# First modulation of a decoder layer: weights of two d tiles in one load, the first pair's products on TensorE

## The chip, the cores and the metric

The kernel runs on one core of one Trainium2 chip. The metric is the device time of one execution in microseconds. TensorE multiplies matrices and transposes, VectorE and ScalarE work elementwise, GpSimd too but without access to the PSUM banks, and SyncE (SP) only issues transfers. Each engine takes its instructions in order.

## What is computed

One layer of a decoder with 1024 tokens, width 1024, f32, with a modulation of both norms:

```python
c_act = jax.nn.silu(c)
mod = (c_act @ mod_w[l] + mod_b[l])[:, None, :]
sh1, sc1, g1, sh2, sc2, g2 = jnp.split(mod, 6, axis=-1)
h = _rmsnorm(x, norm1_g[l]) * (1.0 + sc1) + sh1
z = h @ w_in[l]
q, k, v, f_logit, u = jnp.split(z, splits, axis=-1)
...   # attention with forget gates, pooling, output projection
h = _rmsnorm(x, norm2_g[l]) * (1.0 + sc2) + sh2
x = x + g2 * _conv_ffn(h, ...)
return _rmsnorm(x, final_g)
```

The change lies in how `sh1` and `sc1` (the columns g = 0 and g = 1 of `mod_w`, 1024 each) reach the first `h`, and in the order of the work around that.

## The kernel before

Accuracy of f32 is had with pairs: a matrix is split in a high part (a cast on ScalarE) and a low part (raw minus high), and each product is three matmuls, high by high, low by high, high by low.

The start-up stage (lines 123 to 456) turns x into `HI` and `LO`, the pair of the transposed, modulated `h`, and computes the first three column blocks of the projection (`psu`, one q, one k and one pooling block). x comes in eight tiles of 128 tokens (`load_x`). Per pair of tiles: squares on ScalarE (`norm_sq`), a root (`norm_pair`), scaling with VectorE for one tile and GpSimd for the other (`norm_scale`), 16 transposes into four PSUM banks (`norm_T(t)`, groups g of two d tiles), and copies into `xT[j]` (`norm_evac(t, g)`). There are eight d tiles j of 128 columns.

The modulation of d tile j is a column of `A1` (scale) and of `H1` (shift). `load_mod_d(j)` loads its weights as four transfers of 256 KB into two buffers `mst` (128 rows by 4 k by 2 g by 128 columns, so rows of 512 B in memory). `mod_dve(j, k0, k1)` multiplies and adds them over k on VectorE into `accd`, one operation of 256 elements a row for each k; `mod_end(j)` sums over the 128 partitions with two products of two columns on TensorE, and two activations on ScalarE write A1 and H1. For the tiles 0 and 1 the last two k (`NV` = 6) are products on TensorE instead (`mod_pe`).

`make_hT(j, ch)` makes one token half ch of tile j: ScalarE writes HI and an f32 copy `hf`, and `LOb` is their difference, on GpSimd for all tiles but the last (`LOJ` = 7) and the first half of tile 0. `su_mm(j, ch)` is the nine matmuls of 512 columns that use it. `su_split` splits the weights of these blocks (`sur` into `suh` and `sul`, the low part on GpSimd), in two halves of four k. `wv_gen` splits the weights of v (`wvr`, low part on GpSimd) for the next stage, `v_gen`, whose products are `psv`.

In this stage the order on TensorE, VectorE, ScalarE, GpSimd and SP is the order of the code (`manual_schedule`: `order`, `startup` and `loads`). `startup` ends at line 456; behind it a planner orders VectorE, ScalarE and GpSimd by its own timeline, and TensorE keeps the written order to the end. PSUM has eight banks, all under one tag (`B1`); six of them hold `psu` once both halves have begun. `warm` issues small products without use.

The loop over the d tiles (line 436) begins a tile's first product, ends the modulation of the next, sums the one after, and makes HI and LO of the next:

```python
for j in range(KT):
    if j > 0: su_mm(j, 0, (0,))
    if j + 1 < KT:
        mod_end(j + 1)
        if j + 2 < KT: mod_dve(j + 2)
    if j > 0: su_mm(j, 0, (1, 2))
    ...   # make_hT(j + 1, 0), make_hT(j + 1, 1), su_split, wv_gen
    su_mm(j, 1)
```

Of the kernel before, what the change touches and what calls it, by code (L numbers as in the profile page):

```python
# [50 lines left out]
def kernel(  # L51
# [115 lines left out]
    modv = mod_w.rearrange("(k p) (g j b) -> g j p k b", p=128, g=6, b=128)  # L167
    mst = {}

    def load_mod_d(j):  # L170

        st = []
        for hf in range(2):
            m = (Tqk if j < 4 else Tmx)("mst", (128, 4, 2, 128), F32)
            for g in range(2):
                nc.sync.dma_start(out=m[:, :, g, :], in_=modv[g, j][:, hf * 4:hf * 4 + 4, :])
            st.append(m)
        mst[j] = st
# [19 lines left out]
    for j in range(1, 4):  # L198
        load_mod_d(j)
# [75 lines left out]
    def norm_evac(t, g):  # L275
        for j in (2 * g, 2 * g + 1):
            if j not in xT:
                xT[j] = (Tp if j < 5 else Tv if j < 7 else Tqk)(f"xT{j}", (128, 1024), F32)
            o = xT[j][:, t * 128:(t + 2) * 128]
            i_ = nps[t, g][:, (j % 2) * 256:(j % 2) * 256 + 256]  # L280
            if g % 2 == 0 or t > 3:
                nc.scalar.copy(out=o, in_=i_)
            else:
                nc.vector.tensor_copy(out=o, in_=i_)
# [6 lines left out]
    def mod_pe(j):  # L291

        pm = pms[j] = B1("pm")
        for g in range(2):
            for k in range(NV, KT):
                mm(pm[:, 0:2], lhsT=mst[j][1][:, k % 4, g, :], rhs=cact[:, k, 1 - g:3 - g],
                   start=g == 0 and k == NV, stop=False)

    def mod_dve(j, k0=0, k1=KT):
        if k0 == 0:  # L300
            accs[j] = Ts2("accd")
        acc = accs[j]
        for k in range(k0, k1):
            m = mst[j][k // 4][:, k % 4]
# [6 lines left out]
    def mod_end(j):  # L311
        fresh = j not in pms
        pm = B1("pm") if fresh else pms[j]
        for g in range(2):
            mm(pm[:, 0:2], lhsT=accs[j][:, g, :], rhs=one_z[:, 1 - g:3 - g], start=fresh and g == 0, stop=g == 1)
# [4 lines left out]
    def Ts2(name):  # L320
        return Tpt(name, (128, 2, 128), F32)

    def make_hT(j, ch, eng):
# [20 lines left out]
    def wv_gen(vh, r):  # L344
# [3 lines left out]
        for k0 in range(0, KT, g):  # L348
# [5 lines left out]
            while a < k1:  # L354
# [4 lines left out]
                nc.gpsimd.tensor_sub(out=ll, in0=raw, in1=f(hh))  # L359
# [29 lines left out]
    for g in range(4):  # L389
        norm_evac(0, g)  # L390
    warm(WARM[2])
    norm_T(2)
    norm_sq(4)
# [3 lines left out]
    for g in range(4):  # L397
        norm_evac(2, g)
    warm(WARM[3])
    norm_T(4)  # L400
    norm_sq(6)
    norm_sq(7)
    mod_dve(0, 0, 4)
    norm_evac(4, 0)
    norm_evac(4, 1)
    norm_pair(6)
    norm_scale(6)
    warm(WARM[4])
    mod_pe(0)
    mod_dve(0, 4, NV)  # L410
    norm_evac(4, 2)
    norm_evac(4, 3)
    for i in range(3):
        su_split(i, 0, nc.gpsimd)
    norm_T(6, (0, 1))
    norm_evac(6, 0)
    mod_end(0)
    norm_T(6, (2, 3))
    mod_dve(1, 0, 4)
    make_hT(0, 0, nc.vector)  # L420
    for g in range(1, 4):
        norm_evac(6, g)
    su_mm(0, 0, (0,))
    mod_dve(1, 4, NV)
    mod_pe(1)
    su_mm(0, 0, (1, 2))
    make_hT(0, 1, nc.gpsimd)
    for i in range(3):
        su_load(i, 1)
    for j in range(4, KT):  # L430
        load_mod_d(j)
# [4 lines left out]
    for j in range(KT):  # L436
        if j > 0:
            su_mm(j, 0, (0,))
        if j + 1 < KT:
            mod_end(j + 1)  # L440
            if j + 2 < KT:
                mod_dve(j + 2)
        if j > 0:
            su_mm(j, 0, (1, 2))
        if j + 1 < KT:
            eng = nc.gpsimd if j + 1 < LOJ else nc.vector
            make_hT(j + 1, 0, eng)
            make_hT(j + 1, 1, eng)
        for i in {1: (0, 1), 2: (2,)}.get(j, ()):
            su_split(i, 1, nc.gpsimd)  # L450
# [1312 lines left out]
```

## Time and profile before

| | us |
|---|---|
| median of 3 runs (1107.68 to 1109.01) | 1108.06 |
| the profiled execution, its own time | 1108.36 |
| its span, first to last instruction | 1106.6 |
| TensorE busy in the span | 1071.8 |
| VectorE busy | 877.4 |
| ScalarE busy | 590.8 |
| GpSimd busy | 184.9 |

The profile names engines PE (TensorE matmuls), PEld (its weight loads), DVE (VectorE), ACT (ScalarE), POOL (GpSimd) and SP. An instruction is named by its line, operation and `out<-in` with the names of the tiles. Matmuls are pipelined, so the busy time of one is longer than its distance to the next. Times in the rows are microseconds from the start of the span.

### The profile page before, as it was taken

The numbers are of one execution on the slowest core, as the hardware profiler recorded it, in microseconds if no ns is written. First come the engines' busy times: TensorE is split into PE (matmuls) and PEld (weight loads), VectorE is DVE, ScalarE is ACT, GpSimd is POOL, SyncE is SP. The second block draws the span as 40 slices with busy tenths as digits, with TensorE's granted clock in tenths as the row PEclk, the third lists the DMA queues.
The fourth block names the chain that finished last, engine by engine and source line by source line (L and its number), as shares of the span: only waits on it lengthen the run. The fifth ranks groups of instructions, "written<-read, shape, count | busy, mean of one in ns | idle before, by whom it ended". The sixth has DMA issues, their size and how long they took to land.

```text
span 1106.6 us, 15492 instructions
## 1 busy us (share of the span) xinstructions
PE 1071.8 (97%) x5400; PEld 894.6 (81%) x5400; DVE 877.4 (79%) x1562; ACT 590.8 (53%) x1085; POOL 184.9 (17%) x185
## 2 busy tenths in 40 slices
PE   7899999989999999999999999999999999999997
PEld 7689887768877788888888888888888888788885
DVE  6987578878668645889877777788887869969986
ACT  7664445545667605766544545555655545425434
POOL 4565243336256510000000000000000000000000
PEclk9899999999999999999999999999999999999999
DMA  9953265371333612205322232324334289992474
GB/s 297 293 185 91 52 207 145 91 202 45 64 66 104 219 39 92 80 20 140 108 95 77 76 95 74 133 99 168 117 135 139 88 282 381 387 338 86 144 247 152
DMA packets 138389, 161.90 MB, mean 146 GB/s; under 512 B 9597, under 2 KB 94409, under 8 KB 138313
## 3 DMA queue, kind: packets, MB, share of 16 engines
q1 hardware_dynamic: 133561, 143.89, 41.8%
q10 hardware_dynamic: 4752, 17.04, 3.9%
q8 instruction: 42, 0.69, 0.3%
q14 instruction: 34, 0.28, 0.1%
HBM read 126.26 MB, written 30.45 MB: 142 GB/s over the span
## 4 chain that ended last, share of the span: by engine, by line
PE 76%; DVE 13%; DMA 4%; ACT 3%; issue 3%; POOL 0%; SPq 0%; DVEq 0%; ACTq 0%; POOLq 0%
PE ua L1297 19%; PE ub L1297 10%; PE da L1297 9%; PE db L1297 6%; PE z L923 5%; PE uc L1297 5%; DMA mrow<-in_mod_w_dram 3%; PE po L986 2%; PE po L984 2%; PE po L988 2%; PE psu L337 2%; PE pv L829 2%; DVE P L775 2%; PE psv L661 1%; PE psv L662 1%
## 5 line engine op out<-in xcount | busy, mean ns | idle before, releaser
L1262 ACT CAST uh<-wraw 128x512 fp32r<-128x512 f32 x128 | 79.2, 622 | 122.1 <-PE ua L1297 78.2
L1263 DVE TENSOR_TENSOR ul<-wraw,uh 128x512 fp32r<-128x512 f32 x128 | 87.5, 684 | 15.8 <-PE ub L1297 10.4
L1297 PE MATMUL ua<-t,uh 128*128 128x512 f32 x320 | 98.7, 390 | 0.3 <-ACT u L1341 0.3
L786 ACT ACTIVATE P<-P,mn 128x128 f32<-128x128 f32 (+3 forms) x64 | 49.7, 777 | 76.0 <-DVE mn L775 41.9
L793 POOL TENSOR_SCALAR P<-P,ri 128x128 f32<-128x128 f32 (+3 forms) x64 | 65.7, 1028 | 136.7 <-DVE ri L792 129.2
L810 DVE TENSOR_TENSOR pl<-tpp,ph 128x512 fp32r<-128x512 f32 (+1 forms) x80 | 50.7, 634 | 34.1 <-ACT ph L809 33.8
L1297 PEld LDWEIGHTS ua<-t,uh 128*128 128x128 f32 x320 | 59.9, 188 | 13.2 <-ACT u L1341 0.7
L1297 PE MATMUL da<-th,sl 128*128 128x512 f32 (+1 forms) x166 | 63.6, 383 | 1.6 <-DVE sl L1615 1.6
L775 DVE CUSTOM_DVE_ANT_0 P<-s,Fb 128x512 f32<-128x512 f32 (+2 forms) x96 | 50.2, 552 | 17.6 <-PE s L773 10.3
L1297 PE MATMUL da<-th,sh 128*128 128x512 f32 (+1 forms) x166 | 63.4, 382 | 0.5 <-DVE sv L1629 0.5
L1297 PE MATMUL da<-tl,sh 128*128 128x512 f32 (+1 forms) x166 | 63.3, 381 | 0.0
L1297 PE MATMUL ua<-t,ul 128*128 128x512 f32 x160 | 62.3, 389 | 0.0
L1297 PE MATMUL ua<-HIb,uh 128*128 128x512 f32 x160 | 62.2, 389 | 0.0
L1297 PE MATMUL ua<-LOb,uh 128*128 128x512 f32 x160 | 62.2, 389 | 0.0
L1297 PE MATMUL ua<-HIb,ul 128*128 128x512 f32 x160 | 62.2, 389 | 0.0
L923 PE MATMUL z<-HIb,wh 128*128 128x512 f32 x144 | 60.6, 421 | 0.0
L1374 DVE SCALAR_TENSOR_TENSOR tvv<-cv,colB,tvv 128x1023 f32<-128x1023 f32 (+1 forms) x44 | 56.2, 1279 | 5.2 <-ACT tvv L1372 4.8
L923 PE MATMUL z<-LOb,wh 128*128 128x512 f32 x144 | 59.4, 412 | 0.0
L923 PE MATMUL z<-HIb,wl 128*128 128x512 f32 x144 | 59.0, 409 | 0.0
L1374 DVE SCALAR_TENSOR_TENSOR tg<-cg,colB,tg 128x1023 f32<-128x1023 f32 (+1 forms) x44 | 56.3, 1279 | 1.0 <-ACT tg L1372 0.9
L809 ACT CAST ph<-tpp 128x512 fp32r<-128x512 f32 (+1 forms) x80 | 43.1, 540 | 20.5 <-PE tpp L802 9.7
L1297 PE MATMUL db<-th,sh 128*128 128x512 f32 x132 | 51.3, 389 | 0.0
(322 smaller groups left out, 3158.4 us busy)
## 6 DMA issues: line engine op xcount, KB each, us to landing
wraw<-in_ffn_up_dram SPq DMA_DIRECT2D x88, 256.0 KB, 3.4
mrow<-in_mod_w_dram SPq DMA_DIRECT2D x32, 512.0 KB, 8.3
actd<-tvv ACTq DMA_DIRECT2D x22, 512.0 KB, 2.7
ra<-in_ffn_down_dram SPq DMA_DIRECT2D x44, 256.0 KB, 5.3
x<-in_x_dram SPq DMA_DIRECT2D x16, 512.0 KB, 5.0
mst<-in_mod_w_dram SPq DMA_DIRECT2D x32, 256.0 KB, 5.4
ra<-actd SPq DMA_DIRECT2D x29, 256.0 KB, 5.7
rb<-in_ffn_down_dram SPq DMA_DIRECT2D x22, 256.0 KB, 5.2
```

Of the source, the lines that this page charges most:

```text
L337: mm(su_ps[i, ch], lhsT=su_w[i][w][:, j, :], rhs=act[j][:, ch * 512:(ch + 1) * 512], start=j == 0 and n == 0, stop=j == KT - 1 and n == 2)
L775: nc.vector.tensor_tensor_reduce(out=pt[:, n0:n1], in0=s[:, 0:n], in1=Fb[:, n0:n1], scale=1.0, scalar=3.0e38, op0=ALU.add, op1=ALU.min, ac ...
L786: nc.scalar.activation(out=pt, in_=pt, func=AF.Exp, scale=-1.0, bias=mn, accum_out=rs)
L793: nc.gpsimd.tensor_scalar(out=pt, in0=pt, scalar1=ri, scalar2=1.0, op0=ALU.mult, op1=ALU.mult)
L809: nc.scalar.copy(out=ph[:, 0:W], in_=tp[:, 0:W])
L810: nc.vector.tensor_sub(out=pl[:, 0:W], in0=tp[:, 0:W], in1=f(ph[:, 0:W]))
L829: mm(o, lhsT=V, rhs=x_[:, sl], start=b == 0 and not lo, stop=bool(lo and diag and kb == 1))
L923: mm(t[ch], lhsT=w[:, k, :], rhs=act[kk][:, ch * 512:(ch + 1) * 512], start=i == 0 and m == 0 and p0, stop=i == 1 and m == 3 and p1)
L1262: nc.scalar.copy(out=h, in_=src)
L1263: nc.vector.tensor_sub(out=l, in0=src, in1=f(h))
L1297: mm(*a, skip_group_check=True, **k)
L1374: nc.vector.scalar_tensor_tensor(out=t[:, sh:S], in0=s[:, 0:S - sh], scalar=cw_col[w][:, jj:jj + 1], in1=t[:, sh:S], op0=ALU.mult, op1=ALU ...
```

## The change

The first modulation is loaded for two d tiles at once: `load_mod_d(jp)` makes four buffers of the same size as before, 2 k by 2 g by 256 columns, two transfers of 256 KB each, with rows of 1 KB. The number of transfers and bytes stays. The first pair (tiles 0 and 1) has no sums on VectorE any more: all eight k are products on TensorE. For the other pairs VectorE sums six k in operations of 512 elements, and TensorE does two k and the sum over partitions, per tile. GpSimd does none of the splits of this stage: LO, the `sul` and the first `wvl` are subtractions on VectorE. Transposes are copied out of PSUM in another order and partly by another engine, tokens 0 to 511 first; two of the `warm` calls go; `su_mm(0, 0)` comes before the last transposes. The loop begins with tile 1 and ends the modulation of two tiles at every odd j. The diff:

```diff
@@ -164,18 +164,15 @@
         nc.scalar.copy(out=h, in_=raw)
         eng.tensor_sub(out=l, in0=raw, in1=f(h))
 
-    modv = mod_w.rearrange("(k p) (g j b) -> g j p k b", p=128, g=6, b=128)
+    modv = mod_w.rearrange("(k p) (g j b) -> g j p k b", p=128, g=6, b=256)
     mst = {}
 
-    def load_mod_d(j):
-
-        st = []
-        for hf in range(2):
-            m = (Tqk if j < 4 else Tmx)("mst", (128, 4, 2, 128), F32)
+    def load_mod_d(jp):
+
+        for q in range(4):
+            m = mst[jp, q] = (Tqk if jp < 2 else Tmx)("mst", (128, 2, 2, 256), F32)
             for g in range(2):
-                nc.sync.dma_start(out=m[:, :, g, :], in_=modv[g, j][:, hf * 4:hf * 4 + 4, :])
-            st.append(m)
-        mst[j] = st
+                nc.sync.dma_start(out=m[:, :, g, :], in_=modv[g, jp][:, 2 * q:2 * q + 2, :])
 
 
     wv_raw = {}
@@ -195,8 +192,7 @@
     load_mod_d(0)
     for i in range(3):
         su_load(i, 0)
-    for j in range(1, 4):
-        load_mod_d(j)
+    load_mod_d(1)
 
     def warm(n):
 
@@ -272,36 +268,39 @@
 
     xT = {}
 
-    def norm_evac(t, g):
+    def norm_evac(t, g, dve):
         for j in (2 * g, 2 * g + 1):
             if j not in xT:
                 xT[j] = (Tp if j < 5 else Tv if j < 7 else Tqk)(f"xT{j}", (128, 1024), F32)
             o = xT[j][:, t * 128:(t + 2) * 128]
             i_ = nps[t, g][:, (j % 2) * 256:(j % 2) * 256 + 256]
-            if g % 2 == 0 or t > 3:
+            if dve:
+                nc.vector.tensor_copy(out=o, in_=i_)
+            else:
                 nc.scalar.copy(out=o, in_=i_)
-            else:
-                nc.vector.tensor_copy(out=o, in_=i_)
 
     A1 = cp.tile([128, 8], F32, name="A1")
     H1 = cp.tile([128, 8], F32, name="H1")
 
     pms, accs = {}, {}
 
-    def mod_pe(j):
-
-        pm = pms[j] = B1("pm")
-        for g in range(2):
-            for k in range(NV, KT):
-                mm(pm[:, 0:2], lhsT=mst[j][1][:, k % 4, g, :], rhs=cact[:, k, 1 - g:3 - g],
-                   start=g == 0 and k == NV, stop=False)
-
-    def mod_dve(j, k0=0, k1=KT):
+    def mod_pe(j, k0=NV, k1=KT, last=False):
+
+        fresh = j not in pms
+        if fresh:
+            pms[j] = B1("pm")
+        b = slice((j % 2) * 128, (j % 2) * 128 + 128)
+        for k in range(k0, k1):
+            for g in range(2):
+                mm(pms[j][:, 0:2], lhsT=mst[j // 2, k // 2][:, k % 2, g, b], rhs=cact[:, k, 1 - g:3 - g],
+                   start=fresh and k == k0 and g == 0, stop=last and k == k1 - 1 and g == 1)
+
+    def mod_dve(jp, k0, k1):
         if k0 == 0:
-            accs[j] = Ts2("accd")
-        acc = accs[j]
+            accs[jp] = Ts2("accd")
+        acc = accs[jp]
         for k in range(k0, k1):
-            m = mst[j][k // 4][:, k % 4]
+            m = mst[jp, k // 2][:, k % 2]
             if k == 0:
                 nc.vector.tensor_scalar(out=acc, in0=m, scalar1=cact[:, 0, 1:2], scalar2=None, op0=ALU.mult)
             else:
@@ -309,18 +308,19 @@
                                                op0=ALU.mult, op1=ALU.add)
 
     def mod_end(j):
-        fresh = j not in pms
-        pm = B1("pm") if fresh else pms[j]
-        for g in range(2):
-            mm(pm[:, 0:2], lhsT=accs[j][:, g, :], rhs=one_z[:, 1 - g:3 - g], start=fresh and g == 0, stop=g == 1)
+        pm = pms[j]
+        if j > 1:
+            b = slice((j % 2) * 128, (j % 2) * 128 + 128)
+            for g in range(2):
+                mm(pm[:, 0:2], lhsT=accs[j // 2][:, g, b], rhs=one_z[:, 1 - g:3 - g], start=False, stop=g == 1)
         nc.scalar.activation(out=A1[:, j:j + 1], in_=pm[:, 1:2], func=AF.Identity, scale=n1_col[:, j:j + 1],
                              bias=nb[:, j:j + 1])
         nc.scalar.activation(out=H1[:, j:j + 1], in_=pm[:, 0:1], func=AF.Identity, bias=mb_col[:, j:j + 1])
 
     def Ts2(name):
-        return Tpt(name, (128, 2, 128), F32)
-
-    def make_hT(j, ch, eng):
+        return Tpt(name, (128, 2, 256), F32)
+
+    def make_hT(j, ch, eng=nc.vector):
         sl = slice(ch * 512, (ch + 1) * 512)
         raw = xT[j][:, sl]
         t = (Tpt if j < 5 else Twr if ch == 0 else Tmx)("hf", (128, 512), F32)
@@ -356,7 +356,7 @@
                 raw = wv_raw[vh][a // 4][:, a % 4:a % 4 + b - a, :]
                 hh, ll = h[:, a - k0:b - k0, 0:256], l[:, a - k0:b - k0, 0:256]
                 nc.scalar.copy(out=hh, in_=raw)
-                nc.gpsimd.tensor_sub(out=ll, in0=raw, in1=f(hh))
+                (nc.vector if vh == 0 else nc.gpsimd).tensor_sub(out=ll, in0=raw, in1=f(hh))
                 a = b
             if vh == 0:
                 rf = wf_raw[:, k0:k1, :]
@@ -386,68 +386,74 @@
     norm_sq(3)
     norm_pair(2)
     norm_scale(2)
-    for g in range(4):
-        norm_evac(0, g)
     warm(WARM[2])
     norm_T(2)
+    norm_evac(0, 0, True)
+    norm_evac(0, 1, True)
     norm_sq(4)
     norm_sq(5)
     norm_pair(4)
     norm_scale(4)
-    for g in range(4):
-        norm_evac(2, g)
-    warm(WARM[3])
-    norm_T(4)
     norm_sq(6)
     norm_sq(7)
-    mod_dve(0, 0, 4)
-    norm_evac(4, 0)
-    norm_evac(4, 1)
     norm_pair(6)
     norm_scale(6)
-    warm(WARM[4])
-    mod_pe(0)
-    mod_dve(0, 4, NV)
-    norm_evac(4, 2)
-    norm_evac(4, 3)
+    norm_evac(2, 0, True)
+    norm_evac(2, 1, True)
+    norm_evac(0, 2, False)
+    norm_evac(0, 3, False)
+    mod_pe(0, 0, 4)
+    mod_pe(1, 0, 4)
+    norm_T(4)
+    norm_evac(4, 0, False)
+    mod_pe(0, 4, KT, True)
+    mod_end(0)
+    mod_pe(1, 4, KT, True)
+    make_hT(0, 0)
+    mod_end(1)
     for i in range(3):
-        su_split(i, 0, nc.gpsimd)
+        su_split(i, 0, nc.vector)
+    norm_evac(2, 2, True)
+    norm_evac(2, 3, True)
     norm_T(6, (0, 1))
-    norm_evac(6, 0)
-    mod_end(0)
+    su_mm(0, 0)
+    norm_evac(6, 0, False)
+    make_hT(0, 1)
+    norm_evac(4, 1, True)
+    norm_evac(4, 2, True)
+    norm_evac(4, 3, True)
     norm_T(6, (2, 3))
-    mod_dve(1, 0, 4)
-    make_hT(0, 0, nc.vector)
-    for g in range(1, 4):
-        norm_evac(6, g)
-    su_mm(0, 0, (0,))
-    mod_dve(1, 4, NV)
-    mod_pe(1)
-    su_mm(0, 0, (1, 2))
-    make_hT(0, 1, nc.gpsimd)
+    make_hT(1, 0)
+    norm_evac(6, 1, False)
+    norm_evac(6, 2, False)
+    norm_evac(6, 3, False)
+    make_hT(1, 1)
+    mod_dve(1, 0, 3)
+    su_mm(0, 1)
     for i in range(3):
         su_load(i, 1)
-    for j in range(4, KT):
-        load_mod_d(j)
+    load_mod_d(2)
+    load_mod_d(3)
     load_wv(0)
     nc.sync.dma_start(out=wf_raw, in_=w_in[:, 3 * AW:3 * AW + 8].rearrange("(k p) c -> p k c", p=128))
     w0 = []
     w0g = wv_gen(0, w0)
-    for j in range(KT):
-        if j > 0:
-            su_mm(j, 0, (0,))
+    for j in range(1, KT):
+        odd = j % 2 == 1
+        if odd and j + 1 < KT:
+            mod_dve((j + 1) // 2, 3, NV)
+        su_mm(j, 0)
+        if odd and j + 1 < KT:
+            for jj in (j + 1, j + 2):
+                mod_pe(jj)
+                mod_end(jj)
         if j + 1 < KT:
-            mod_end(j + 1)
-            if j + 2 < KT:
-                mod_dve(j + 2)
-        if j > 0:
-            su_mm(j, 0, (1, 2))
-        if j + 1 < KT:
-            eng = nc.gpsimd if j + 1 < LOJ else nc.vector
-            make_hT(j + 1, 0, eng)
-            make_hT(j + 1, 1, eng)
-        for i in {1: (0, 1), 2: (2,)}.get(j, ()):
-            su_split(i, 1, nc.gpsimd)
+            make_hT(j + 1, 0)
+            make_hT(j + 1, 1)
+        if not odd and j + 2 < KT:
+            mod_dve(j // 2 + 1, 0, 3)
+        for i in {2: (0, 1), 3: (2,)}.get(j, ()):
+            su_split(i, 1, nc.vector)
         if j == 6:
             next(w0g, 0)
         su_mm(j, 1)
```

## Rows read from the trace of the kernel before

**Rows 1.** The page: TensorE's busy time, share and instructions; its clock in 40 slices.

```profile
PE 1071.8 (97%) x5400; PEld 894.6 (81%) x5400; DVE 877.4 (79%) x1562; ACT 590.8 (53%) x1085; POOL 184.9 (17%) x185
...
PEclk9899999999999999999999999999999999999999
```

**Rows 2.** Stretches: us, busy PE, PEld, DVE, ACT, POOL, granted clock, DMA share, GB/s.

```profile
20.00:24.00 4.00, 2.92 (x29) 2.61 (x27) 3.79 (x10) 3.36 (x11) 2.56 (x2) 0.96 1.11 285
24.00:28.00 4.00, 3.59 (x16) 3.08 (x15) 3.89 (x5) 2.46 (x7) 3.14 (x3) 0.50 1.14 286
...
52.00:56.00 4.00, 4.00 (x11) 3.13 (x11) 3.82 (x7) 3.44 (x6) 1.67 (x2) 0.50 0.92 264
```

**Rows 3.** Waits of PE, 28 to 130 us: us in total, times, longest.

```profile
PE pm L315 <- DVE accd L308: 4.6, 2, 3.7
```

**Rows 4.** The chain that ended last, two pieces of it: start, us, what.

```profile
52.03 6.99 PE psu L337 x18
...
59.36 4.20 PE psu L337 x18
```

**Rows 5.** Timeline, TensorE at the end of the stage.

```profile
74.57 0.84 PE L337 MATMUL psu<-LOb,suh 128*128 128x512 f32 x3
75.25 0.85 PE L337 MATMUL psu<-HIb,sul 128*128 128x512 f32 x3
...
78.22 0.36 PE L661 MATMUL psv<-wvl,HIb 128*128 128x264 f32 x1 [0.71 <-DVE wvl L365]
```

**Rows 6.** Tiles accd and macc: count, duration ns min, median, max; starts.

```profile
L308 DVE SCALAR_TENSOR_TENSOR accd<-mst,cact,accd x52: 478/485/1601, 19.0 to 66.1; 128x256 f32<-128x256 f32 x52
...
L306 DVE TENSOR_SCALAR accd<-mst,cact x8: 343/348/1359, 18.6 to 60.6; 128x256 f32<-128x256 f32 x8
...
L536 DVE SCALAR_TENSOR_TENSOR macc<-mrow,cact,macc x28: 1256/1284/3204, 75.1 to 251.2; 128x1024 f32<-128x1024 f32 x28
L534 DVE TENSOR_SCALAR macc<-mrow,cact x4: 749/893/1626, 72.7 to 222.1; 128x1024 f32<-128x1024 f32 x4
```

**Rows 7.** Timeline, sums on VectorE: start, us from first to last, line, what.

```profile
43.68 7.22 DVE L308 SCALAR_TENSOR_TENSOR accd<-mst,cact,accd 128x256 f32<-128x256 f32 x7
```

**Rows 8.** Timeline, ScalarE and VectorE at the last d tile.

```profile
68.54 0.35 ACT L316 ACTIVATE A<-pm,colA 128x1 f32<-128x1 f32 x1 [1.12 <-PE pm L315]
...
69.07 0.82 ACT L327 ACTIVATE HIb<-xT,H,A 128x512 fp32r<-128x512 f32 x1
...
69.79 0.80 ACT L328 ACTIVATE hf<-xT,H,A 128x512 f32<-128x512 f32 x1
...
70.63 0.69 DVE L329 TENSOR_TENSOR LOb<-hf,HIb 128x512 fp32r<-128x512 f32 x1 [2.97 <-ACT hf L328]
```

**Rows 9.** Timeline, the start: transposes, warm, evacuations, products, casts.

```profile
10.32 0.33 PE L271 MATMUL tp<-ident,x 128*128 128x128 f32 x1 [0.36 <-DVE x L261]
...
13.84 1.92 PE L271 MATMUL tp<-ident,x 128*128 128x128 f32 x16
...
15.59 1.00 PE L205 MATMUL warm<-identb 128*128 128x128 bf16 x15
...
17.32 1.41 DVE L284 COPY xT<-tp 128x256 f32<-128x256 f32 x4
...
20.69 1.00 PE L296 MATMUL pm<-cact,mst 128*128 128x2 f32 x8
...
21.33 1.72 ACT L164 CAST suh<-sur 128x512 fp32r<-128x512 f32 x3
...
28.69 1.70 PE L296 MATMUL pm<-cact,mst 128*128 128x2 f32 x8
```

**Rows 10.** Stretches by transfer: x; mst and sur; wvr. Last column GB/s.

```profile
4.00:12.00 8.00, 6.98 (x88) 6.50 (x89) 3.56 (x20) 6.57 (x14) 1.59 (x1) 1.00 1.01 402
...
28.00:46.00 18.00, 16.98 (x72) 14.04 (x71) 17.36 (x24) 13.56 (x28) 10.12 (x8) 0.84 1.18 287
49.00:51.00 2.00, 0.00 (x0) 0.00 (x0) 1.93 (x4) 0.00 (x0) 0.58 (x1) 0.99 1.10 344
```

## Prediction

> **What bounds the kernel now.** The page comes first: the matmul row of TensorE is busy 97% of the span and its clock is full in all slices but a few [rows 1]. So time can be won or lost only where TensorE waits, runs at the lower clock or gets more to do, and the change touches only the stage before the `psv` products of `v_gen`. The table of stretches shows that stage to be the weak one: granted clock 0.96 from 20 to 24 us, 0.50 (1.2 GHz, not 2.4) from 24 to 28 and from 52 to 56, and VectorE busy for 3.8 to 3.9 of each 4 us [rows 2]. The waits of TensorE say what is late: 4.6 us for `accd`, the modulation sums on VectorE, one of these waits 3.7 us long [rows 3]. The chain of waits prices the clock: 18 `psu` products take 6.99 us after the long wait and 4.20 later [rows 4]; at the end of the stage groups of three stand 0.68 apart [rows 5], so the 9 of one `su_mm(j, ch)` cost 2.06 us at the full clock and, doubled, 4.1 at the half one. VectorE is late because of GpSimd: `accd` is 0.485 us an operation at the median [rows 6], and seven beside GpSimd's splits take 7.22, not 3.5 [rows 7]. `psu` runs out near 76.0, and `psv` then stops 0.7 us for `wvl` [rows 5]. I call **76.7 us** the end of the stage: behind it stands the same work in the same TensorE order, so this is the number to compare.
>
> **The change, part by part.** *GpSimd leaves the stage* except for scaling x. That takes away the stretching of [rows 7], over 15 us of VectorE's time, but the splits come to VectorE: 16 `LOb` and 6 `sul` of the same shape at 0.69 us [rows 8].
>
> *Sums for two d tiles.* An operation is now 128x512. The trace has 256 elements (0.485 and 0.348 us) and 1024 (1.256 and 0.749) [rows 6]; on a straight line 512 costs 0.74, and 0.48 for the first. Bounds: 0.485 if width were free, 0.97 if it were two old ones; the line is nearest. A pair has six: 0.48 + 5 x 0.74 = **4.2 us**, for three pairs; the first has none.
>
> *Products on TensorE.* The two `mod_pe` calls of before are four products each and show as eight records: an f32 product is two passes. Eight records take 1.00 us at the full clock and 1.70 to 2.0 at the half one [rows 9], so a product costs 0.24 or 0.49. The first pair now has 32 products, 7.7 us, in four runs of 1.93; each other pair has 8 and 4 of `mod_end`, 2.9 us. Sum 16.4 us against 24 products and 5.8 before; 25 `warm` products go, some 1.7. TensorE has 9 us more to do. Before, 48 of the 66 us from its first transpose at 10.3 [rows 9] to 76.0 were work at the full clock (64 transposes 7.7, products 5.8, `warm` 1.7, `psu` 33); 17 were waits and half clock.
>
> *Loads.* Rows of 1 KB for 512 B. The stretch with only `wvr`, of 1 KB rows, moves 344 GB/s against 287 where `mst` flows [rows 10]. x (4.2 MB at 402 GB/s from about 3 us) is over at 13.5; half the first pair (1.05 MB) lands near 17.6 with a microsecond of latency, all near 20.7, `sur` 23.5, the second pair 30, the others 39 and 45. SP stands at `su_load(i, 1)` until the splits have read `sur`, with the last two pairs and `wvr` queued behind it; even 8 us of that leave the third pair in time. So only the first half pair is on the path: 0.6 us won. The Trainium skill, page "DMA: Bandwidth & Descriptors", section Specifications, gives 512 B as the least transfer for line rate. By that rule the old rows lose nothing, the new ones win nothing, and the sum would rise by 0.6 us; the rows here disagree with it, 287 against 344.
>
> *The new start.* ScalarE no longer evacuates between the squares, so x is scaled some 4 us sooner and is not what TensorE waits for. But TensorE has a row of its own: two runs of products 17.6 to 21.5, transposes of x4, x5 (1.92) to 23.4, then the second run for tile 0. In the kernel before the clock fell to half about 24, when products of two columns, few transposes and waits had gone before [rows 2, 9]; I take the same here. That run ends at 26.7 and tile 1's at 30.6, transposes at 32.5. ScalarE: A, H by 27.4, HI, hf by 28.9, A, H of tile 1 by 31.3 (before the `sur` casts in its queue), casts by 33.0 (0.57 each [rows 9]). VectorE subtracts by 34.1 and evacuates (0.353 each [rows 9]) by 35.5. Here is a wait for banks: five of eight hold unread transposes and two take those of x6, x7, so the third `psu` bank comes with `norm_evac(2, 2)`, 34.8. `su_mm(0, 0)` ends at 37.8, the last transposes at 39.4, `norm_evac(6, 3)` at 40.0, HI and hf of (1, 1) at 41.4, LO 42.1, six sums at **46.3**: T2.
>
> *The loop.* `startup` fixes VectorE's order as written, and `mod_dve` of the next pair stands behind the `LOb` of all four `make_hT` of this pair, which wait for ScalarE; behind the sums wait `mod_end` and the next `make_hT`. The period is a ring: from the sums' end 2.2 us for `mod_end`, `mod_pe`, `mod_end`; A, H 0.6; four `make_hT`, 8 x 0.715 = 5.8 [rows 8]; the last LO 0.7; sums 4.2; and two `su_split` on VectorE, 1.4, in the first turn, one cast on ScalarE, 0.6, in the second. First turn 15.0: T4 = 61.3. TensorE has four `su_mm` and 2.9 of products in it, 11.2, and waits some 4.6 in one piece; a wait of 3.7 was followed by half clock before [rows 2, 3], so the hand-over of the second turn takes 4.3: 16.2, T6 = 77.5. Then 2.2 and five `su_mm`, 10.3, with 0.2 for LO of tile 7: end **90.2**. Before, the work behind the last modulation (68.5) was less than four `su_mm`.
>
> *The value weights.* Their splits on VectorE (near 0.95 and 0.2 us behind the last LO) are ready before the last `su_mm` ends, so the stop of 0.7 goes; it is in the 76.7.
>
> **Sum.** 90.2 - 76.7 = +13.5 us. The profiled execution took 1108.36 (span 1106.6 and 1.76 around it), so 1121.9 on its scale; the median of the runs shown, 1108.06, lies 0.3 lower: **1121.6 us**, 1.2% slower. A measurement of this kernel can tell about 0.2%, 2.2 us, from no change.
>
> **The rivals.** *Faster (1106 to 1104):* the ring doesn't close. TensorE's own work after 10.3 is 7.7 of transposes, 16.4 of products and 33 of `psu`: 67.4 is the floor of the end, 9 us under now. With T2 at 40 and the sums worked off in VectorE's gaps of 0.74 us between two LO, what is left at T2 is 13 `su_mm` (26.8) and 8 of products: end 74.8, -1.9, and the order that the planner draws anew in attention could add as much. Place: VectorE's queue after `make_hT(2, 0)`; the point is T6 under 62. For it: over 15 us of stretching vanish; against: the order is written out, and sums come after all four LO. Chance 0.12.
>
> *The same (1108):* sums near 0.5, full clock throughout and a ring of 12.3 and 11.6: T6 64.5, end 77. Chance 0.10. That the change doesn't do what it says (1 KB rows at 287 GB/s) is 0.6 us and within any case.
>
> *The ring, start at the full clock (1117):* the same steps with 1.93 a run: products end 27.3, T2 42.0, end 85.9, +9.2; with no half clock later either 83.7, 1115. Chance 0.25. *Ring and half clock from 24 (1121.6):* the forecast, 1119 to 1124. Chance 0.38. *Half clock from 20 on (1126.5):* the products of two columns don't hold the clock at all, the transposes of x4, x5 take 3.9 and T2 is 51; end 95, +18. Chance 0.15.
>
> **How the numbers follow.** The forecast is the likeliest case. The range leaves a tenth on each side: from 1106.5, between the first two rivals, to 1126.5, the middle of the last. Faster 0.12, same 0.10, slower 0.25 + 0.38 + 0.15 = 0.78.
>
> **What would show it.** `accd` near 0.74 us each, none long; `pm` products with 64 records before the loop, and the clock beside them (0.50 from 24, or 1.00); the first nine `psu` between 32 and 38 with a wait in them; waits of TensorE for `accd` of 1 to 5 us ahead of tiles 2, 4 and 6, which stand near 46, 61 and 77; `psv` without a stop, near 90. If sums run between the LO of one pair, or `psu` begins at 27 and goes through, the forecast is wrong and the time lower. If TensorE's waits in attention shift by more than 2 us in all, the stage's difference isn't the kernel's.

## The result and the profile after

The changed kernel took 1123.82 us (median of 4 runs, 1117.94 to 1127.14) against 1107.87 for the kernel before on the same chip: ratio 1.0139, 95% interval 1.0093 to 1.0186, so slower, by some 16 us. Taken again later on another occasion (`a0` below) it was 1125.34. Its own runs differ by 9 us, where those of before differ by 2.8 (by 3.0 to 7.1 in the four later sessions), and the granted clock over the span goes with them: 0.986 in the run of 1117.94, 0.983 at 1122.19, 0.981 at 1125.45, 0.979 at 1127.14. The profile named "after" is the run of 1117.94, the quickest of the four; the profile of `a0` is one of 1126.07. Both are read here.

The page of after, its lines as in [rows 1]: TensorE has 11.6 us more of busy time, VectorE 17 less, GpSimd 32 less.

```profile
PE 1083.4 (97%) x5463; PEld 905.9 (81%) x5463; DVE 860.2 (77%) x1553; ACT 588.0 (53%) x1075; POOL 152.6 (14%) x162
...
PEclk8889999999999999999999999999999999999999
```

The stretches of 4 us in after (columns as in [rows 2]):

```profile
16.00:20.00 4.00, 2.24 (x17) 2.09 (x17) 2.31 (x9) 2.52 (x7) 1.92 (x2) 1.00 1.09 347
20.00:24.00 4.00, 4.00 (x22) 4.00 (x22) 0.58 (x2) 0.00 (x0) 0.24 (x1) 0.55 1.17 311
24.00:28.00 4.00, 4.00 (x25) 4.00 (x23) 0.00 (x0) 0.65 (x2) 0.00 (x0) 0.60 1.09 348
28.00:32.00 4.00, 4.00 (x31) 3.82 (x30) 1.03 (x2) 3.29 (x8) 0.00 (x0) 0.83 0.24 69
...
64.00:68.00 4.00, 4.00 (x11) 3.13 (x10) 2.07 (x4) 4.00 (x7) 0.00 (x0) 0.50 0.09 25
...
92.00:96.00 4.00, 3.92 (x18) 3.64 (x19) 3.87 (x6) 1.16 (x3) 2.30 (x2) 0.57 0.33 59
```

VectorE, busy 3.8 of each 4 us before, now stands almost still from 20 to 28, while the data flow at 311 and 348 GB/s and TensorE works at little more than half clock. The waits of TensorE from 28 to 100 us (us in total, times, longest):

```profile
PE pm L315 <- DVE accd L307: 4.1, 2, 2.4
PE psv L667 <- DVE wvl L365: 2.4, 2, 1.9
PE psu L337 <- ACT xT L280: 0.8, 1, 0.8
```

The timeline of TensorE in after: the second run of the first pair's products, then the products that end a modulation of two tiles (T2, T4 and T6 of the prediction), then the stop of `psv`:

```profile
26.40 4.02 PE L295 MATMUL pm<-cact,mst 128*128 128x2 f32 x32
...
45.80 0.61 PE L315 MATMUL pm<-cact,accd 128*128 128x2 f32 x4 [2.44 <-DVE accd L307]
...
60.12 0.61 PE L315 MATMUL pm<-cact,accd 128*128 128x2 f32 x4 [1.70 <-DVE accd L307]
...
74.41 0.61 PE L315 MATMUL pm<-cact,accd 128*128 128x2 f32 x4
...
90.14 0.39 PE L667 MATMUL psv<-wvl,HIb 128*128 128x264 f32 x1 [1.89 <-DVE wvl L365]
```

How the profiled executions of all kernels pass the same places is in this table: the starts of the first `psu`, the first `psv`, the first product `z` after `v_gen`, the first `po` after attention, and the last `da`, near the end. Each ratio is against runs of the kernel before on the same chip, taken with it. The profiled run is one of the runs and not their median: it is the longest in a0, e1, e3, e4 and e8, and the shortest in after, e5, e6 and e11. One execution of e5, of 3301.66 us, is left out of its row.

| kernel | median (range), us | ratio (95%) | profiled | psu | psv | z | po | last da |
|---|---|---|---|---|---|---|---|---|
| before | 1107.87 (1106.22–1109.01) | 1 | 1108.36 | 27.3 | 76.1 | 126.5 | 345.2 | 1098.4 |
| after | 1123.82 (1117.94–1127.14) | 1.0139 (1.0093–1.0186) | 1117.94 | 31.7 | 86.8 | 140.9 | 356.7 | 1108.2 |
| a0 | 1125.34 (1123.35–1126.07) | 1.0146 (1.0131–1.0161) | 1126.07 | 35.6 | 95.0 | 146.7 | 362.0 | 1116.3 |
| e1 | 1115.70 (1114.40–1121.21) | 1.0060 (1.0043–1.0077) | 1121.21 | 34.3 | 90.2 | 144.1 | 359.4 | 1111.7 |
| e2 | 1117.12 (1116.02–1118.59) | 1.0076 (1.0061–1.0091) | 1116.38 | 29.1 | 84.3 | 138.4 | 356.2 | 1106.9 |
| e3 | 1124.33 (1119.23–1126.16) | 1.0133 (1.0106–1.0159) | 1126.16 | 34.1 | 93.3 | 146.6 | 363.6 | 1116.4 |
| e4 | 1113.85 (1112.68–1117.75) | 1.0049 (1.0033–1.0065) | 1117.75 | 29.2 | 85.2 | 139.1 | 357.4 | 1108.1 |
| e5 | 1121.91 (1120.81–1122.08) | 1.0109 (1.0092–1.0125) | 1120.81 | 34.2 | 89.4 | 143.5 | 358.6 | 1111.0 |
| e6 | 1099.63 (1097.61–1101.58) | 0.9910 (0.9892–0.9929) | 1097.61 | 25.9 | 70.0 | 120.4 | 336.4 | 1088.2 |
| e7 | 1105.97 (1104.12–1109.45) | 0.9969 (0.9958–0.9980) | 1106.22 | 27.3 | 77.2 | 127.6 | 345.6 | 1096.3 |
| e8 | 1099.38 (1096.65–1100.53) | 0.9906 (0.9882–0.9931) | 1100.53 | 27.4 | 72.8 | 123.1 | 340.2 | 1090.9 |
| e9 | 1102.15 (1100.10–1103.46) | 0.9936 (0.9915–0.9958) | 1101.16 | 27.3 | 71.6 | 122.0 | 340.0 | 1091.6 |
| e10 | 1105.77 (1103.35–1106.81) | 0.9969 (0.9955–0.9982) | 1105.77 | 27.4 | 73.5 | 124.3 | 343.2 | 1096.3 |
| e11 | 1119.67 (1116.19–1124.90) | 1.0113 (1.0077–1.0150) | 1116.19 | 31.7 | 86.9 | 138.7 | 353.5 | 1106.5 |

Of after's profile it says: `psu` begins 4.4 us late, `psv` 10.7 and `z` 14.4; attention (z to po) then gives 2.9 back and the last stage 1.7, so that 9.8 are left. In `a0` the same places are 8.3, 18.9, 20.2, 16.8 and 17.9 late. The stage before `psv` is where the time goes, in both.

### The profile page after: what moved, and what is told of

It is laid out like the page before. It is cut to its first block, busy times and chain, and to the rows that moved or that the text cites. A ratio compares the mean times of both kernels' runs of the same rounds, so it can differ in the third digit from the quotient of the medians.

```text
span 1115.9 us, 15565 instructions
## 1 busy us (share of the span) xinstructions
PE 1083.4 (97%) x5463; PEld 905.9 (81%) x5463; DVE 860.2 (77%) x1553; ACT 588.0 (53%) x1075; POOL 152.6 (14%) x162
## 4 chain that ended last, share of the span: by engine, by line
PE 71%; DVE 13%; DMA 7%; ACT 4%; issue 3%; SPq 0%; POOL 0%; DVEq 0%; ACTq 0%; POOLq 0%
PE ua L1303 19%; PE ub L1303 10%; PE da L1303 8%; PE db L1303 5%; PE uc L1303 5%; PE z L929 4%; DMA mrow<-in_mod_w_dram 3%; PE po L990 2%; PE po L992 2%; PE po L994 2%; PE pv L835 2%; DVE P L781 1%; DMA mst<-in_mod_w_dram 1%; PE tpp L812 1%; PE psv L667 1%
## 5 line engine op out<-in xcount | busy, mean ns | idle before, releaser
L799 POOL TENSOR_SCALAR P<-P,ri 128x128 f32<-128x128 f32 (+3 forms) x64 | 65.8, 1029 | 134.8 <-DVE ri L798 126.3
```

Source lines behind the costliest of these rows:

```text
L799: nc.gpsimd.tensor_scalar(out=pt, in0=pt, scalar1=ri, scalar2=1.0, op0=ALU.mult, op1=ALU.mult)
```

## The experiments

### The changed kernel again (a0), and what each part of it costs

> The changed kernel itself, to see how far its runs lie apart (1117.9 to 1127.1 in four runs, where the kernel before kept to 1106.2 to 1109.0) and where the spread sits. Theory of the clock: granted clock and time go together, 0.001 of mean clock is 2.2 us at half clock and costs 1.1 us, and the stretches at half clock that come and go lie before 100 us (the products of two columns at the start, the stop of psv). Rival: the spread lies in attention, where the planner's order is the same each time but waits on transfers differ; then the first psv comes at the same time (86 to 88 us) in a slow run, and waits between 130 and 420 us grow.

The spread has its place. The stretches of `a0`:

```profile
16.00:20.00 4.00, 2.54 (x14) 2.40 (x15) 2.39 (x9) 2.53 (x7) 2.00 (x2) 0.80 1.10 347
20.00:24.00 4.00, 4.00 (x20) 4.00 (x21) 0.51 (x2) 0.00 (x0) 0.17 (x1) 0.50 1.17 310
24.00:28.00 4.00, 4.00 (x21) 4.00 (x21) 0.00 (x0) 0.65 (x2) 0.00 (x0) 0.50 1.10 348
28.00:32.00 4.00, 4.00 (x20) 4.00 (x20) 0.00 (x0) 1.21 (x3) 0.00 (x0) 0.50 0.23 66
```

and two rows of its timeline, TensorE:

```profile
27.31 6.83 PE L295 MATMUL pm<-cact,mst 128*128 128x2 f32 x32
...
49.87 1.01 PE L315 MATMUL pm<-cact,accd 128*128 128x2 f32 x4 [2.34 <-DVE accd L307]
```

The same 32 records that took 4.02 us in after take 6.83 here, at a granted clock of 0.50 from 20 to 40 us. Between the two profiles 3.9 us lie ahead of the first `psu` and 4.3 more ahead of `psv` (again half clock in the hand-overs: 0.64 and 0.50 from 48 to 56, 0.50 from 80 to 84). The instructions are the same in both; what decides in which run the clock comes back near 26 us is not settled by these runs. The Trainium skill, page "TensorE: Matmul & The Clock Gate", section "What's actually happening", says that the number of products at the low clock differs from run to run of one kernel; these two traces agree, 0.60 against 0.50 from 24 to 28.

### The ring of the sums (e1)

```diff
-        if odd and j + 1 < KT:
-            mod_dve((j + 1) // 2, 3, NV)
+        if j == 1:
+            mod_dve(1, 3, NV)
...
+        jp = (j + 3) // 2
         if j + 1 < KT:
             make_hT(j + 1, 0)
+            if jp < 4:
+                mod_dve(jp, 0, 2) if odd else mod_dve(jp, 4, NV)
             make_hT(j + 1, 1)
-        if not odd and j + 2 < KT:
-            mod_dve(j // 2 + 1, 0, 3)
+            if odd and jp < 4:
+                mod_dve(jp, 2, 4)
```

> The six sums of the next pair go between the make_hT of this pair on VectorE (two behind each of three halves) instead of behind all four. Nothing else changes. Theory of the ring: the wait of TensorE for accd ahead of tile 4 (1.7 us at 60.1) goes, the next modulation comes near 58.4, the half clock of 60 to 68 us (some 2.7 us) does not occur, and the first psv comes 3 to 5 us sooner than 86.8. Rival, TensorE is full with its own products anyway: first psv sooner by less than 1 us, and LO, now behind sums, becomes what psu waits for.

9.6 us less than `a0` by the medians, where I had expected 3 to 5 at the first `psv`. Its profile is of its longest run, which has the same long start at half clock as that of `a0`:

```profile
26.01 6.83 PE L295 MATMUL pm<-cact,mst 128*128 128x2 f32 x32
```

Beside the profile of `a0` it is 4.9 us shorter, 3.5 of them between the first `psu` and the first `psv`, so the sums behind the four LO cost about what I had expected. The other four runs of e1 are another 5.0 to 6.8 us quicker, at a granted clock of 0.986 to 0.988 where the profiled one has 0.983. Of the three waits for `accd` in `a0` one is left, 2.3 us ahead of tile 2, and a wait for `sul` comes out that the ring had hidden; the one for `suh` is in `a0` too, and `psv` still waits 2.4 us for `wvl` (waits of TensorE, 28 to 100 us, the others):

```profile
PE pm L315 <- DVE accd L307: 2.3, 1, 2.3
PE psu L337 <- ACT suh L164: 1.3, 1, 1.3
PE psu L337 <- DVE sul L165: 1.0, 1, 1.0
```

How much of the 9.6 is the shorter ring, how much the clock that the shorter waits keep up, and how much the clock at the start, which differs between runs of one kernel and which this edit doesn't touch, can't be told apart by it.

### The first pair back on VectorE (e2), and both (e4)

```diff
-    mod_pe(0, 0, 4)
-    mod_pe(1, 0, 4)
+    mod_dve(0, 0, NV)
     norm_T(4)
     norm_evac(4, 0, False)
-    mod_pe(0, 4, KT, True)
+    mod_pe(0)
+    mod_pe(1)
     mod_end(0)
-    mod_pe(1, 4, KT, True)
```

> The first pair is summed on VectorE like the others (six k there, two k and the partition sum on TensorE), which VectorE has time for, being idle from 20.6 to 30.8 us. 64 records of products before the loop become 24. Theory, the products of the first pair hold up the start: A of tile 0 comes near 25.5 to 26 instead of 28.7, first psu near 29, and psv 2 to 4 us sooner. Rival, the start is set by the splits of sur and the banks: A sooner, but the first psu and psv at the same time within 1 us.

In this run `mod_end` sums over the partitions for the tiles 0 and 1 too. Beside the profile of after, `psu` and `psv` come 2.6 and 2.5 us sooner, within the 2 to 4 expected, and the profile is 1.6 us shorter. By the medians it is 8.2 us less than `a0`: the long start of `a0` has gone as well, and the runs lie within 2.6 us, at a granted clock of 0.984 to 0.985. VectorE has the time for these six sums: it stood still there. The clock is no better (0.50 from 24 to 32), TensorE simply has less to do at that clock: 16 records of products and 8 of `mod_end` in place of 64. Both edits together:

> Both edits that helped: the sums of the next pair between the make_hT, and the first pair summed on VectorE. Alone they took the changed kernel from 1125.3 to 1115.7 and to 1117.1, that is 9.6 and 8.2 us. Theory, ring and first products are separate costs: together 15 to 18 us, near 1107.5 to 1110, level with the kernel before. Rival, both gains are the same half clock, got back once: together 10 to 12, 1113 to 1115, with the clock at 0.5 still from 22 to 34 us.

11.5 us less than `a0`, where the two alone give 9.6 and 8.2. They don't add up, as the rival had it, and 1.0049 of before remains.

### The value weights sooner (e3) and the warm products back (e5)

`if j == 6` of the loop becomes `if j in (5, 6)`:

> The first two groups of value weights are split one d tile sooner (behind make_hT of tiles 6 and 7 instead of tile 7 and the end). Theory, the stop of psv after ten products (1.89 and 0.52 us of waiting for wvl, and half clock at 92 to 96 us, some 1.5 us more) comes from their place in VectorE's queue behind macc: it goes, and the kernel is 3 to 4.5 us faster than the changed one. Rival, VectorE has too much to do there and LO of tile 7 comes later by as much: first psv later by 2 to 3 us, no gain.

No gain (1124.33). `wvl` is ready, and the stop of `psv` has only changed its cause:

```profile
PE psv L666 <- DVE qb L511: 1.8, 1, 1.8
```

`psv` needs a bank that `psu` holds until VectorE has taken it out, so VectorE's queue is what is late at this place, and `wvl` only one of the things in it. One thing that makes it late is GpSimd: a `wvl` of 16 elements a row takes VectorE 2.38 us here, at 93.4, beside a GpSimd subtraction of 2.96 us; the same takes 0.16 us in after with GpSimd idle.

In e5 `warm(15)`, `warm(10)` and `warm(10)` stand around the first two runs of products:

> 35 small warm products (2.3 us at the full clock) come back into the changed kernel, around the first 16 products of two columns, ahead of the transposes of x4 and x5. Theory of the clock: waiting for mst and products of two columns let the clock fall near 20 us and it stays at half until 41 in most runs; with warm products between, the granted clock is above 0.8 from 20 to 28 us, A of tile 0 comes some 3 us sooner than in the repeated run of the changed kernel, and the median is 3 to 6 us under 1125.3. Rival, the start hangs on the landing of mst and the ScalarE queue: the added work costs its 2 us and the median is 1125 to 1128.

3.4 us less than `a0`, runs within 1.3 us. That lies in the theory's 3 to 6, but not by its mechanism, and the ratio can't be told from that of after (their intervals overlap). The clock falls all the same, to 0.50 from 20 to 28:

```profile
16.00:20.00 4.00, 2.98 (x28) 2.66 (x26) 2.46 (x9) 2.52 (x7) 2.05 (x2) 0.94 1.09 346
20.00:24.00 4.00, 4.00 (x26) 4.00 (x26) 0.43 (x2) 0.00 (x0) 0.09 (x1) 0.50 1.17 311
```

`warm` products at these places do not hold the clock up.

### GpSimd off, wide loads, in the old order (e6, e7, e8)

In the kernel before, `nc.gpsimd` becomes `nc.vector` in both `su_split` calls, in `make_hT(0, 1)` and for all tiles of the loop:

> One part of the change alone, in the kernel before: all subtractions of LO and sul of the start go from GpSimd to VectorE (the wvl stay). Theory: VectorE gains 19 operations of 0.69 us (13.1 us) and loses the stretching of accd beside GpSimd (some 15 us); accd comes down to 0.49 to 0.5 each, and the time is within 3 us of the kernel before. Rival, the stretching is what holds the stage: 4 us or more faster; the other one, LO waits in VectorE's order behind whole sums: 5 us or more slower.

My theory falls and the rival holds: 0.991, faster than both kernels. The timeline of VectorE in e6 shows what it is. Seven sums in 3.61 us where [rows 7] has 7.22, though two LO now stand behind them:

```profile
35.76 3.61 DVE L308 SCALAR_TENSOR_TENSOR accd<-mst,cact,accd 128x256 f32<-128x256 f32 x7
39.28 1.29 DVE L329 TENSOR_TENSOR LOb<-hf,HIb 128x512 fp32r<-128x512 f32 x2
```

and the waits of TensorE from 28 to 100 us come in small pieces, where [rows 3] has one of 3.7:

```profile
PE pm L315 <- DVE accd L308: 4.0, 6, 1.4
```

No wait is followed by half clock any more: in the stretches of e6 it is 0.57 from 24 to 28 and 1.00 in all from 28 on, where before has 0.50 from 52 to 56, behind the long wait.

```profile
24.00:28.00 4.00, 4.00 (x21) 3.59 (x20) 3.89 (x9) 3.76 (x12) 0.00 (x0) 0.57 1.09 286
28.00:32.00 4.00, 4.00 (x24) 3.45 (x24) 3.19 (x8) 3.13 (x7) 0.00 (x0) 1.00 1.09 273
...
52.00:56.00 4.00, 4.00 (x19) 3.33 (x19) 3.78 (x8) 3.44 (x6) 0.00 (x0) 1.00 1.01 287
```

The waits themselves add up to nearly as much as before, 4.0 us against 4.6. What the low clock takes can be estimated from the stretches: TensorE's busy time in each, times what its granted clock lacks to 1, comes to 7.9 us in before and 1.7 in e6, summed from 12 to 100 us. The difference of 6.2 is about all that `psv` gains. 6.1 us of the profile's gain stand at `psv` and at `z`, 2.7 come in attention, 1.4 in the last stage. The Trainium skill, page "SBUF — State Buffer", section "Who interferes with whom", says that an operation of VectorE with two inputs in SBUF and one of GpSimd that reads there exclude each other for a whole instruction; the trace agrees: a sum of 0.485 us becomes up to 1.60 beside GpSimd [rows 6], and seven of them lose 3.6 us [rows 7] beside 5.4 us of GpSimd's work (43.7 to 50.9 us).

In e7 the kernel before loads `mst` as the change does (`b=256`, two k a buffer) and uses the half of a buffer that a tile needs, in its own order:

```diff
-    modv = mod_w.rearrange("(k p) (g j b) -> g j p k b", p=128, g=6, b=128)
+    modv = mod_w.rearrange("(k p) (g j b) -> g j p k b", p=128, g=6, b=256)
...
-            m = mst[j][k // 4][:, k % 4]
+            m = mst[j // 2, k // 2][:, k % 2, :, (j % 2) * 128:(j % 2) * 128 + 128]
```

> The other part alone, in the kernel before: mst in rows of 1 KB for two d tiles, the sums and products as before on slices of 256 elements. Theory of the prediction, loads are worth about 1 us at the first tile and nothing later: within 1.5 us of the kernel before; the transfers move 340 to 350 GB/s instead of 287. As tile 0 waits for a pair (2.1 MB) instead of one tile, it may start up to 2 us later. Rival, the loads bind the stage before (the chain shows one wait for mst): 3 us or more faster.

3.5 us less, as much as the rival asked, but not in its place: `psv` and `z` come 1.1 later than before in the profile, although the loads run at 347 GB/s from 16 to 20 us where before has 288, and at up to 353 later. In the stage itself the wide loads win nothing in this profile. What it gains stands behind, 0.7 us in attention and 2.5 in the last stage, where the profile of before waits 1.6 us for `sl`, a split on VectorE; that wait comes and goes between executions of one kernel, as shown below, so that the cause of the 3.5 us stays open.

> The kernel before with both gains: all LO and sul subtractions of the stage on VectorE, and the first modulation loaded in 1 KB rows for two d tiles. Alone they gave -9.1 us (ratio 0.991) and -3.5 us (0.9969). My theory: they don't add up, since with GpSimd off VectorE is the bound at 8 sums of 0.485 and two LO of 0.69, 5.3 us a tile, and the data are there in time: 1099 to 1100, ratio 0.991, first psu near 25.9. Rival: they are on different pieces of the path and add up: 1096, ratio 0.988, first psu 1 to 3 us sooner.

They don't add up, as the theory had it: 1099.38, e6 again. `psu` even begins at 27.4, not 25.9, with the clock at 0.55 and 0.50 from 24 to 32.

### Products on TensorE in the old order (e9, e10)

In e9 each tile from 2 on gets `mod_pe` ahead of `mod_end`, and VectorE sums `NV` = 6 of eight k:

> As the one with both gains, and the d tiles 2 to 7 too have two of eight k as products on TensorE, as the tiles 0 and 1 have; VectorE sums six k a tile, 2.9 us and not 3.9. Theory: TensorE's waits for accd in the loop (4.0 us in six with GpSimd off) go, and 24 products of 0.24 us come, 5.8 us: 1 to 3 us slower than with both gains alone, no accd waits, clock full. Rival: the waits cost more than they show and the clock is steadier: 2 to 4 us faster than with both gains alone.

2.8 us slower than e8 by the medians, within the theory's 1 to 3, but the intervals of the two ratios overlap. No wait for `accd` is left, and the clock is full from 36 on. `psv` begins 1.2 us sooner in it, not later as the theory's mechanism would have it; the 1.8 us that it then loses in the profiles come behind `z`.

In e10 `mod_pe` of the tiles 0 and 1 takes all eight k, the `mod_dve` of both go, and `mod_end` has no product for them:

> As the one with both gains, and the tiles 0 and 1 have all eight k as products on TensorE (32 products, none with accd), where before eight were: the part of the change that the other runs have not priced in the old order. Theory: products of two columns cost TensorE 20 more x 0.24 us = 4.8 us at the full clock, 9.8 at the half one, and the half clock comes with them between 20 and 30: 5 to 9 us slower than with both gains alone, first psu 3 to 6 us later. Rival: TensorE has idle time there and VectorE is freed of 12 sums, 5.8 us: within 1 us or faster.

6.4 us slower than e8, within the theory's 5 to 9, but not by its mechanism: the first `psu` is where it was, 27.4, and `psv` and `z` are 0.7 and 1.2 later. 1.8 more come in attention and 2.4 in the last stage. So the first pair's products cost this order about a microsecond in the stage itself, clock low though it is (0.57 from 24 to 28, 0.50 from 32 to 36); what makes the rest isn't shown.

### LO on GpSimd again in the changed kernel (e11)

In the loop `make_hT(j + 1, ...)` gets `nc.gpsimd` up to tile 6:

> The changed kernel with one edit: LO of the d tiles 2 to 6 is subtracted on GpSimd again (1.34 us each in the kernel before), so that in VectorE's queue the sums of the next pair no longer stand behind the LO of this one; the sul and wvl subtractions stay on VectorE. My theory (the ring goes through VectorE's queue): the sums run beside make_hT, even stretched to 1.4 us each they take 8.4 us of the 11 that four su_mm and the products last, and TensorE's waits for accd go: 8 to 11 us faster than the changed kernel repeated (1125.3), 1114 to 1117, psv from 84 or sooner. Rival (stretching costs VectorE in the ring what it cost in the old order): the sums take as long beside GpSimd as behind the LO, the waits for accd stay at 3 us or more in all, and the time is within 3 us of 1125.

Neither: 1119.67, 5.7 below `a0` by the medians, though the intervals of the ratios overlap, with waits for `accd` of 4.3 us in all and the first `psv` where after has it (86.9). The clock of its profile at the start is that of after, so the two can be laid side by side: T4 59.6 and T6 73.1 against 60.1 and 74.4, half a microsecond and 1.3 won. The tile `accd` says why (its operations, as in [rows 6]; then what VectorE, idle, waited for ahead of it, us and times):

```profile
L307 DVE SCALAR_TENSOR_TENSOR accd<-mst,cact,accd x15: 739/752/1671, 41.9 to 72.3; 128x512 f32<-128x512 f32 x15
L305 DVE TENSOR_SCALAR accd<-mst,cact x3: 473/481/485, 41.4 to 66.8; 128x512 f32<-128x512 f32 x3
...
  POOL LOb L329: 5.3, 1
```

`accd` and the `hf` of a tile below 5 come from the same four buffers (`Tpt`), taken in the order of the code, which is the likely reason that the sums of the next pair wait for a LO even with VectorE free; no run tests it. Beside GpSimd a sum takes up to 1.67 us; and ahead of the last pair's sums stands a `sul` for which VectorE waits 5.95 us until ScalarE has cast. Taking LO out of VectorE's queue does not open the ring by itself. An order with the sums placed sooner does (e1).

## Why the prediction was right, and where not

**The forecast.** 1121.6 us, range 1106.5 to 1126.5; measured 1123.8, and 1125.3 on the second occasion. The median of the first occasion lies in the likeliest case, ring and half clock from 24; that of the second is nearer the next one, half clock from 20 on.

**The ring holds, step by step.** `accd` is 0.75 us an operation at 512 (0.74 forecast), 0.48 the first. T2, T4 and T6 were 46.3, 61.3 and 77.5; after has 45.8, 60.1 and 74.4, `a0` 49.9, 65.8 and 79.6. `psv` follows T6 by 12.4 us in after (12.7 forecast) and 15.4 in `a0`. With the end of the stage at 90.2, the forecast lies between 86.8 and 95.0; counted with the stops of `psv`, as the 76.7 of before was, between 89.2 and 95.8.

That T2 is right within 0.5 us in after is in part luck. The first runs of products ended at 23.1 (21.5 forecast), since the clock fell sooner, and the transposes of x4, x5 took 3.65 us (1.92); but the clock came back in the second run, so that 32 records took 4.02 us where the forecast left 7.2, and its end came out at 30.4 (30.6). In `a0`, where the clock did not come back, T2 is 3.6 us late.

**The clock was right in kind, wrong in detail.** I had it fall at 24 and one hand-over at half clock, the second. It falls at 20 (0.55) or before (0.80 from 16 in `a0`), and two of the three hand-overs have some of it: in after the first and the second, 0.61 from 48 to 52 and 0.67 and 0.50 from 60 to 68, in `a0` the first and the third. The third of after, ahead of which TensorE did not wait, runs at 1.00. In exchange TensorE's wait ahead of T4 is 1.7 us (0.4 in `a0`), not 4.6, since what it does at half clock it need not wait. The rival "half clock from 20 on", with T2 at 51, end 95 and 1126.5, is `a0` nearly to the number: those two cases were one kernel in different runs, and the split of chances between them was one between executions.

**"Psv without a stop" failed.** It stops for 1.9 and 0.5 us in after and then runs at half clock to 95.6, so that `z` is 14.4 late where `psv` is 10.7. VectorE in after, and below it GpSimd:

```profile
84.43 1.28 DVE L365 TENSOR_TENSOR wvl<-wf_raw,wvh 128x24 fp32r<-128x24 f32 x1
85.63 1.27 DVE L542 SCALAR_TENSOR_TENSOR macc<-mrow,cact,macc 128x1024 f32<-128x1024 f32 x1
86.83 1.01 DVE L359 TENSOR_TENSOR wvl<-wvr,wvh 128x256 fp32r<-128x256 f32 x2
87.77 2.32 DVE L365 TENSOR_TENSOR wvl<-wf_raw,wvh 128x24 fp32r<-128x24 f32 x1
90.01 1.27 DVE L542 SCALAR_TENSOR_TENSOR macc<-mrow,cact,macc 128x1024 f32<-128x1024 f32 x1
91.21 0.68 DVE L359 TENSOR_TENSOR wvl<-wvr,wvh 128x512 fp32r<-128x512 f32 x1
91.81 0.16 DVE L365 TENSOR_TENSOR wvl<-wf_raw,wvh 128x16 fp32r<-128x16 f32 x1
```

```profile
83.98 1.70 POOL L893 TENSOR_TENSOR wl<-wraw,wh 128x512 fp32r<-128x512 f32 x1 [63.73 <-ACT wh L892]
87.21 2.84 POOL L359 TENSOR_TENSOR wvl<-wvr,wvh 128x1024 fp32r<-128x1024 f32 x1 [1.54 <-PE pb L475]
```

Two things make `wvl` late. `macc`, the sums of the next modulation, stands ahead of it: 1.27 us each time. And GpSimd has left the stage, but not this place: it splits weights for what follows, the second half of the value weights among them. Beside that a `wvl` of 24 elements a row takes VectorE 2.32 us and ends at 90.1, with GpSimd; `psv` goes on there. A like one of 16 elements takes 0.16 with GpSimd idle, so that the 1.9 us of the stop are about what this one operation loses. I had priced the splits alone, 0.95 and 0.2 us, as if they had VectorE for themselves. No run moves GpSimd's splits away from there. In after's profile more than the 3.7 us between those two, 4.6, came back behind `z`; in `a0`, where `psv` stops for 0.8 us only, 2.3 did. The two errors offset each other; the sum was not as exact as its last digit.

**Two terms were mis-sized.** GpSimd's leaving was costed as 15 us of stretching against 22 splits of 0.69, nearly a draw; alone it is worth 0.9% (e6), since it ends the long wait and most of the half clock, not since VectorE has less to do: it is busy for 76.5 us from 12 to 100 in e6 and for 77.4 in before. The loads were 0.6 us on the path; in the old order they win nothing at `psv` (e7). Both are hidden in the changed kernel by its own order.

**So the change mixes a gain with a loss.** By e6 the old order without GpSimd is 1099.6; the changed kernel, as `a0`, is 25.7 above that. Of these e1 and e2 take back 9.6 and 8.2 alone and 11.5 together, so less than half is shown by an edit. In the old order the first pair's products cost about 1 us in the stage and 6.4 in all (e10), in the changed one 2.5 in the stage beside the profile of after and 8.2 in all against `a0`, and VectorE stands still beside them there. The 14 us from e4 to e6 are not taken apart by runs: e4 still has `psu` at 29.2, the hand-overs for two tiles at once, and half clock from 24 to 36 and from 44 to 52. The estimate of e6 (busy time times what the clock lacks) says that most of it is the clock: 13.7 us in e4 against 1.7 in e6. It gives 13.0 for after and 19.1 for `a0`, against 7.9 in before: of the 10.7 and 18.9 us by which their `psv` is late, about 5 and 11 are half clock. No run holds the clock up in the changed order.

**Attention shifts.** I had said that more than 2 us there would not be the kernel's, and had named the order that the planner draws anew as what could move it. From `z` to `po` the profiles range over 214.8 (e11) to 218.9 us (e10), but the order is not what differs: by operation and tile name, VectorE, ScalarE and GpSimd run the same sequence there in all fourteen profiles. What makes the difference stays open. From `po` to the last `da` they range over 750.7 (e2) to 754.3 us (a0). There the order on VectorE and ScalarE does differ between kernels; yet after and `a0`, the same kernel, take 751.5 and 754.3. In `a0` TensorE has this wait there, and in after it has none for `sl`:

```profile
PE da L1303 <- DVE sl L1621: 2.9, 2, 2.0
```

So some 3 us behind the stage can come with the execution alone, and a difference of that size between two profiles is not the edit's for that.

## What to carry to other kernels

An operation that waits in a fixed order belongs ahead of what it doesn't depend on: sums whose data had long been there, put behind subtractions that wait for another engine, made a ring of 14 us a turn. Moving work off a helper engine can pay even where the busy engine gets it all, when the two exclude each other and the long wait it makes costs TensorE its clock; it can be tried alone, in the old order, before anything is built on it. And where two executions of one kernel differ by 8 us in one stage and by 3 in another, two profiles with the same clock at the start are compared, or many runs, before a gain of that size is called the edit's.

## What the runs showed of the hardware that I had not expected

- The same instructions at the start of the changed kernel ran at 0.50 through all of 20 to 40 us in one execution, and at 0.55, 0.60, 0.83, 0.50 and 0.82 in the five stretches there in another; 32 records of two columns take 6.83 or 4.02 us.
- In the profiles of all kernels with the new start the granted clock was 0.50 to 0.60 from 24 to 28, with 35 `warm` products more (e5) and whoever summed the first pair (e2). With the old start it was 0.50 to 0.57 there in four, and full in two (e7, e9).
- A sum of 128x512 elements beside GpSimd took up to 1.67 us, alone 0.75; of 128x256 up to 1.60, alone 0.485. At most 0.9 and 1.1 us are lost, about as much for both and less than one of the GpSimd operations (1.34) beside them. A subtraction of 24 elements a row lost 2.2 us beside a longer one (2.32 for some 0.16; GpSimd 2.84) and 1.1 beside one of 1.70. In these rows the loss goes by the length of GpSimd's operation, not of VectorE's own.
